# The order of the projection blocks of a differential attention, and a query norm in two halves

## The chip, the cores and the metric

One core of a Trainium2 chip runs the whole program: TensorE (PE) for matmuls and transposes, with its weight loads (PEld), VectorE (DVE), ScalarE (ACT), GpSimd (POOL), and SyncE (SP), which issues nearly all DMAs. The metric is the device time of one execution in microseconds. Before the change it is 2127.65 us, the median of 3 runs (2126.36 to 2130.23).

## The reference

Two models run one after the other on 256 tokens of width 1024, in float32. The first has two layers, each with an FFN, a mixer (a short convolution in layer 0, a sparse attention in layer 1) and a second FFN. The second takes the first one's tokens (the latents, x) and 256 context tokens (ctx, here xc), and has two layers as well. Only its mixers matter here.

```python
# layer 0: differential attention, for latents and context with the same weights
q, k, v = jnp.split(t @ w_in, 3, axis=-1)            # 3 x 1024 columns
q = rmsnorm(q.reshape(Bt, Lt, 16, 64), q_norm)       # per head of 64
k = rmsnorm(k.reshape(Bt, Lt, 16, 64), k_norm)
q = apply_axial_rope(q, cos, sin)                    # latents alone
k = apply_axial_rope(k, cos, sin)
p = jax.nn.softmax(s, axis=-1)                       # two maps for each of 8 heads
a = p[:, :, 0] - lam * p[:, :, 1]
# layer 1: grouped attention, 8 query heads of 128 on 2 key and value heads
q = rmsnorm(q.reshape(Bt, Lt, 8, 128), q_norm)
s = jnp.einsum('bkgtd,bksd->bkgts', qg, keys) * 128 ** -0.5
```

In both the latents attend to context and latents together; the context of layer 0 attends to itself.

## The kernel before, in words

**Tiling.** 256 tokens are two tiles of 128 (`TT = 2`). Every weight is read in float32 (512 KB for half a slab, `raw_half`, line 237), copied to a rounded high part on ACT (line 246) and a remainder on DVE (line 247); a product is three matmuls (high x high, high x remainder, remainder x high). `a_block` multiplies all tokens with 512 columns: two slabs, eight steps over the inner dimension, two accumulators of 128x512 in PSUM, 48 matmuls. PSUM gives six buffers to tag `ps` and two to `fps`.

**The differential projections** (`second`, phase diff0; the loop at line 1344) are six such blocks. Block b has `part, c = divmod(b, 2)`: b = 0, 1 are queries of heads 0 to 7 and 8 to 15, b = 2, 3 keys, b = 4, 5 values. The order is 0, 4, 2, 1, 5, 3. After block b's matmuls the loop calls `flush()` of the block before, which transposes its normed tiles on PE into `qT` or `kT` (`tr_to`, line 981, and a copy on ACT, line 982), and then `diff_block` for b. A value block is two copies on ACT (line 994). For queries and keys `head_norm` (line 946 on) runs for each token tile: a square on ACT (951), a reduction on DVE (952), the factor (382 on DVE, a power on POOL, 386), for keys the multiplication by it (956, DVE), the two rope products (964, and four pieces at 972, DVE) and their sum (974, DVE); without tables one product with the gain (961). A query's factor is applied later, within the softmax. Behind the loop a stretch of filler runs (`self.fd(self.cfg["diff_mid"])`), then the last `flush`, then `diff_attend`, whose first step multiplies queries and keys (line 1038) and reduces the maximum on DVE (1044).

**The context stream** (`ctx_stream`, line 1179 on) is a generator that does the same for xc without tables, in pieces that the main program takes as filler (`fd`, `fa`): by an estimated time at token boundaries (`boundary`), one piece at a time in the FFNs of layer 1. It has the same order of blocks (line 1198). Its tmp and out buffers hold two tiles each. When its attention is done in program order, keys and values are stored to DRAM (lines 1212, 1213) and read back for the latents (1351, 1352). All of them and the weights go out on SP. The conditioning vectors are filler as well: a 512 KB load, then one or two DVE passes over 1024 columns (line 176).

**The grouped attention** (`second`, phase gqa). Queries are two blocks of four heads. The first is normed (`gqa_q(0, acc)`) beside the second one's matmuls, which are a generator `qgen`, run in part ahead of `gqa_attend` and in part at its step n = 1. `gqa_attend` walks 16 pairs of head and token tile: at step n `stage_a` (scores, line 1125; maximum, 1128, exponential on ACT, 1131; scaling, 1133), then, back in the loop of `second`, whatever stands at n, then `stage_b` of n - 2 (transposes, 1143) and for every second n `stage_c` (line 1151). At n = 1 the rest of `qgen` and the norm of both token tiles are queued, at n = 5 the transposes of both into `qT`. Heads 4 to 7 are used from step 8 on.

**What sets the order.** The engines work in order, each through its own queue. The order of a queue is made when the program is built: a scheduler takes the instructions in program order of priority, but lets a later one go ahead where an earlier one is not ready in its own model of time. Weight splits get a bonus of 36 places (`early`). The kernel's text therefore sets the order around the change only nearly.

Of the kernel before, what the change touches and what calls it, by code (L numbers as in the profile page):

```python
# [25 lines left out]
TT = T // P  # L26
# [44 lines left out]
class Slots:  # L71
# [8 lines left out]
    def next(self):  # L80
        self.i += 1
        return self.parts[(self.i - 1) % len(self.parts)]


class Kern:
# [1093 lines left out]
    def ctx_stream(self):  # L1179
        nc, I = self.nc, self.I  # L1180
        tag = "fps"
        yield "d", 2.0
        self.late_setup()
        diags = [self.norm_r(self.xc, t) for t in range(TT)]
        ab = self.ab(("c", 0, 0), ("c", 0, 1), self.n1(0))
        for _ in self.norm_T(self.xc, diags, ab, tag):
            yield "d", 0.5
        h = self.hT
        qT = self.chunk().rearrange("p (h t) -> p h t", h=8)
        kT = self.chunk().rearrange("p (h t) -> p h t", h=8)  # L1190
        vals = self.chunk().rearrange("p (t d) -> p t d", t=TT)
        rq = self.cp.tile([P, TT, 16], F32, name="rqc")
        tmp, outs = Slots(self.chunk(), 512, 4), None
        outs = Slots(tmp.parts[2:4])
        tmp = Slots(tmp.parts[0:2])
        hk = self.tiles_of(h)
        flush = lambda: None
        for b in (0, 4, 2, 1, 5, 3):
            yield from self.a_block(hk, I["diff_w_in"][2 * b:2 * b + 2], tag, ("p", 2.6))
            flush()  # L1200
            flush = self.diff_block(tmp, outs, self.acc2, b, qT, kT, vals, rq, None, "ps")
        for _ in range(3):
            yield "p", 1.3
        flush()
        hid = self.hid8()
        c = self.chunk()
        es = Slots(c[:, 0:1024], T)
        ats = Slots(c[:, 1024:1536], T)
        ons = Slots(c[:, 1536:2048], P)
        yield from self.diff_attend(es, ats, ons, qT, rq, [(kT, vals)], tag, hid)  # L1210
        self.kvd = self.dram.tile([2, P, 2048], F32, name="kvd")
        nc.sync.dma_start(self.kvd[0], kT.rearrange("p h t -> p (h t)"))
        nc.sync.dma_start(self.kvd[1], vals.rearrange("p t d -> p (t d)"))
        yield "d", 1.7
        G = self.grow(("b", 0, 2), i=1)
        for c in range(2):
            yield from self.a_block(hid, I["diff_w_out"][2 * c:2 * c + 2], tag, ("d", 2.6))
            for t in range(TT):
                self.post2(self.xc, [self.acc2[t]], G, t, [c])
        diags = [self.norm_r(self.xc, t) for t in range(TT)]  # L1220
        ab = self.ab(("b", 0, 3), ("b", 0, 4), self.n2(0), i=1)
        yield "d", 1.7
        G = self.grow(("b", 0, 5), i=1)
        for _ in self.norm_T(self.xc, diags, ab, tag):
            yield "d", 1.5
        h = self.hT
        hid = self.hid4()
        win, wout = I["ffn_w_in"][4 * NF:5 * NF], I["ffn_w_out"][44:55]
        for j in range(0, NF, 4):
            n = min(4, NF - j)  # L1230
            for k in range(n):
                yield from self.ffn_in(h, win[j + k], hid[k], tag, ("d", 2.6))
            for c in range(2):
                yield "d", 1.3
                if n == 4:
                    w = self.slab(tuple(wout[j // 2 + s].rearrange("p (k n) -> p k n", k=2)[:, :, c * 512:(c + 1) * 512]
                                        for s in range(2)))
                elif c == 0:
                    w = self.slab(wout[j // 2])
                acc = [self.ps(tag=tag) for _ in range(TT)]  # L1240
                for k in range(n):
                    if k:
                        yield "d", 1.3
                    if n == 4:
                        ww = tuple(z[:, (k % 2) * 512:(k % 2 + 1) * 512] for z in w[k // 2])
                    else:
                        ww = tuple(z[:, c * 512:(c + 1) * 512] for z in w[k])
                    for t in range(TT):
                        self.a_step([acc[t]], hid[k], ww, k == 0, k == n - 1, t)
                for t in range(TT):  # L1250
                    self.post2(self.xc, [acc[t]], G, t, [c])
        g = self.chunk()
        self.gkT = g[:, 0:1024].rearrange("p (h t) -> p h t", h=2)
        self.gv = g[:, 1024:2048].rearrange("p (k d) -> p k d", k=4)
        diags = [self.norm_r(self.xc, t) for t in range(TT)]
        ab = self.ab(("b", 1, 0), ("b", 1, 1), self.n1(1), i=1)
        for _ in self.norm_T(self.xc, diags, ab, tag):
            yield "d", 0.5
        h = self.hT
        yield from self.a_block(self.tiles_of(h), I["gqa_kv"], tag, ("k", 2.6))  # L1260
        c = self.chunk()
        flush = self.gqa_kv(Slots(c[:, 0:1024], 512), Slots(c[:, 1024:2048], 512), self.acc2, self.gkT, self.gv, 0, None, tag)
        yield "d", 0.5
        flush()
# [67 lines left out]
    def second(self, h):  # L1332
# [8 lines left out]
        tmp, outs = Slots(c0, 512), Slots(c1, 512)  # L1341
        hk = self.tiles_of(h)
        flush = lambda: None
        for b in (0, 4, 2, 1, 5, 3):
            acc = self.block(hk, I["diff_w_in"][2 * b:2 * b + 2])
            flush()
            flush = self.diff_block(tmp, outs, acc, b, qT, kT, vals, rq, tabs, "ps")
# [52 lines left out]
        hk = self.tiles_of(h)  # L1400
        flush = self.gqa_kv(tmp, outs, self.block(hk, I["gqa_kv"]), self.gkT, self.gv, T, tabs, "ps")

        def gqa_q(c, acc):
            pend = []
            for t in range(TT):
                rr = rq[:, t, 4 * c:4 * c + 4]
                o = self.head_norm(tmp, outs, acc[t], 4, 128, self.row("gq"), tabs[0], t, rr, False)
                nc.vector.tensor_scalar(rr, rr, 128.0 ** -0.5, None, op0=ALU.mult)
                pend.append((qT[:, 4 * c:4 * c + 4, t * P:(t + 1) * P], o))

            def flush():
                for dst, o in pend:
                    self.tr_to(dst, o, 4)

            return flush

        acc = self.block(hk, I["gqa_q"][0:2])
        flush()
        flush = gqa_q(0, acc)
        qgen = self.a_block(hk, I["gqa_q"][2:4], "ps", ("q", 0.0))  # L1420
        for n, _ in enumerate(qgen):
# [6 lines left out]
        for n, _ in enumerate(self.gqa_attend(es, ats, qT, rq, self.gkT, self.gv, hid)):  # L1428
            if n == 1:
                for _ in qgen:  # L1430
                    pass
                flush = gqa_q(1, self.acc2)
            if n == 5:
                flush()
            if n in (16, 17):
                next(pg)
        got["acc"] = self.proj(pg)
# [122 lines left out]
```

## Time and profile before

| | before |
|---|---|
| median of 3 runs | 2127.65 us |
| the profiled execution | 2128.49 us |
| its span, first to last instruction | 2126.4 us |
| PE, PEld, DVE, ACT, POOL busy | 94%, 84%, 77%, 51%, 7% |
| bytes moved by DMA | 486.45 MB, 229 GB/s in the mean |
| mean granted clock of TensorE | 0.98 |

Busy shares are those of one profiled execution. A matmul's end is modelled, so a busy PE is not PE at its peak. In a timeline a row has start and duration in us, engine, line, operation, the tile written and the tiles read, and in brackets the idle time of the engine ahead of it with what ended it. The number behind a tile's name tells instances apart. Times count from the span's start.

### The profile page before, as it was taken

The numbers are of one execution on the slowest core, as the hardware profiler recorded it, in microseconds if no ns is written. First come the engines' busy times: TensorE is split into PE (matmuls) and PEld (weight loads), VectorE is DVE, ScalarE is ACT, GpSimd is POOL, SyncE is SP. The second block draws the span as 40 slices with busy tenths as digits, with TensorE's granted clock in tenths as the row PEclk, the third lists the DMA queues.
The fourth block names the chain that finished last, engine by engine and source line by source line (L and its number), as shares of the span: only waits on it lengthen the run. The fifth ranks groups of instructions, "written<-read, shape, count | busy, mean of one in ns | idle before, by whom it ended". The sixth has DMA issues, their size and how long they took to land.

```text
span 2126.4 us, 34675 instructions
## 1 busy us (share of the span) xinstructions
PE 2004.0 (94%) x13158; PEld 1791.2 (84%) x13158; DVE 1628.7 (77%) x2753; ACT 1092.4 (51%) x1773; POOL 142.2 (7%) x188
## 2 busy tenths in 40 slices
PE   6999999999899989999999999989999999999998
PEld 5998897998789878887878999868878899768998
DVE  7878899877886778789978667789879755866454
ACT  4444545443454456657755444548754444555443
POOL 0000201000200000110001000210111000100000
PEclk9999999999999999999999999999999999999999
DMA  8989798988677765563677866564458855414553
GB/s 334 329 310 349 244 324 289 330 296 295 221 278 267 270 203 190 187 232 111 225 240 246 261 234 231 171 208 145 144 173 301 277 185 193 163 50 156 188 184 117
DMA packets 136326, 486.45 MB, mean 229 GB/s; under 512 B 14976, under 2 KB 16480, under 8 KB 135392
## 3 DMA queue, kind: packets, MB, share of 16 engines
q1 hardware_dynamic: 134240, 477.90, 65.7%
q0 software_dynamic: 1728, 6.29, 0.9%
q8 instruction: 103, 1.69, 0.3%
q14 instruction: 63, 0.52, 0.1%
q10 hardware_dynamic: 192, 0.05, 0.0%
HBM read 480.47 MB, written 3.19 MB: 227 GB/s over the span
## 4 chain that ended last, share of the span: by engine, by line
PE 57%; DVE 17%; DMA 11%; issue 6%; ACT 5%; POOL 3%; SPq 0%; DVEq 0%; POOLq 0%; ACTq 0%
DMA raw.ctx.1333_7232<-in_diff_w_in 1%; DMA x<-in_x 0%; DVE x L640 0%; DVE xc L648 0%; DMA raw.a02.1070_5840<-in_ada_w 0%; DMA raw.bffn0.3272_17501<-in_ffn_w_in 0%; ACT chunk.diff0.2769_14964 L1048 0%; DMA raw.a01.584_3153<-in_a_w_in 0%; PE ps.a10.1301_7026 L743 0%; DMA raw.ctx.690_3700<-in_diff_w_in 0%; DMA raw.a01.616_3371<-in_a_w_in 0%; DMA raw.ctx.3148_16958<-in_ffn_w_out 0%; DVE chunk.a11.1878_10047 L886 0%; DVE chunk.a11.1878_10047 L864 0%; DMA raw.a02.924_4991<-in_ada_w 0%
## 5 line engine op out<-in xcount | busy, mean ns | idle before, releaser
L1048 ACT ACT_TABLE_LOAD x15 | 19.2, 1283 | 4.1 <-DVE dst.diff0.2773_14978 L1046 2.2
L340 ACT ACT_TABLE_LOAD x16 | 20.5, 1283 | 0.3
L273 PE MATMUL ps.a00.6_101<-ident,x 128*128 128x128 f32 x4 | 1.1, 427 | 13.6 <-DMA x<-in_x 13.6
L375 POOL DMA_DIRECT2D G.a02.1032_5643<-row.a02.1031_5641 x1 | 0.6, 595 | 180.2 <-DMA row.a02.1031_5641<-diag.a02.1030_5639 180.2
L375 POOL DMA_DIRECT2D G.a12.2539_13777<-row.a12.2538_13775 x1 | 0.6, 595 | 178.5 <-DMA row.a12.2538_13775<-diag.a12.2537_13773 178.5
L273 PEld LDWEIGHTS ps.a00.6_101<-ident,x 128*128 128x128 f32 x4 | 0.7, 216 | 13.6 <-issue 13.6
L375 POOL DMA_DIRECT2D G.bffn2.3890_21467<-row.bffn2.3889_21465 x1 | 0.6, 595 | 171.6 <-DMA row.bffn2.3889_21465<-diag.bffn2.3888_21463 171.6
L401 POOL TENSOR_TENSOR rv.ctx.354_2048<-ss.ctx.352_2044,epsd 128x1 f32<-128x1 f32 x1 | 0.2, 189 | 169.4 <-ACT junk.ctx.351_2043 L394 169.4
L375 POOL DMA_DIRECT2D G.bffn0.3422_18599<-row.bffn0.3421_18597 x1 | 0.6, 595 | 150.9 <-DVE wlo.bffn0.3441_18733 L247 150.9
L733 ACT ACTIVATE chunk.a10.1248_6646<-chunk.kv.1128_6071,cols 128x60 f32<-128x60 f32 x32 | 10.1, 390 | 1.0 <-PE ps.a10.1253_6696 L743 1.0
L333 ACT ACT_TABLE_LOAD x8 | 10.3, 1283 | 0.1
L868 ACT ACT_TABLE_LOAD x7 | 9.0, 1283 | 0.1
L386 POOL TENSOR_TENSOR rr.ctx.1408_7659<-rv.ctx.1407_7657,nhalf 128x8 f32<-128x8 f32 x1 | 2.5, 2477 | 93.1 <-DVE rv.ctx.1407_7657 L382 93.1
L375 POOL DMA_DIRECT2D G.a11.2178_11660<-row.a11.2177_11658 x1 | 0.5, 527 | 121.9 <-DMA row.a11.2177_11658<-diag.a11.2176_11656 121.9
L981 PE MATMUL ps.diff0.2763_14946<-ident,chunk.diff0.2627_14248 128*128 128x128 f32 x4 | 1.1, 435 | 7.1 <-DVE chunk.diff0.2627_14248 L974 7.1
L287 PE MATMUL ps.a00.38_198<-chunk.a00.20_148,chunk.a00.34_188 128*128 128x256 f32 x8 | 3.3, 408 | 4.5 <-ACT chunk.a00.34_188 L299 2.9
L484 ACT CAST chunk.a01.490_2583<-chunk.a01.492_2585 128x256 fp32r<-128x256 f32 x8 | 3.3, 407 | 7.8 <-DVE chunk.a01.492_2585 L676 7.7
L981 PEld LDWEIGHTS ps.diff0.2763_14946<-ident,chunk.diff0.2627_14248 128*128 128x128 f32 x4 | 0.7, 218 | 7.5 <-DVE chunk.diff0.2627_14248 L974 7.5
L287 PEld LDWEIGHTS ps.a00.38_198<-chunk.a00.20_148,chunk.a00.34_188 128*128 128x128 f32 x8 | 2.0, 254 | 5.3 <-ACT chunk.a00.34_188 L299 3.1
L1143 PE MATMUL ps.gqa.3570_19374<-ident,chunk.gqa.3552_19276 128*128 128x128 f32 x4 | 1.1, 435 | 5.1 <-DVE chunk.gqa.3552_19276 L1133 5.1
L386 POOL TENSOR_TENSOR rqc<-rv.ctx.1316_7169,nhalf 128x8 f32<-128x8 f32 x1 | 1.6, 1636 | 61.2 <-DVE rv.ctx.1318_7177 L382 61.2
L1143 PEld LDWEIGHTS ps.gqa.3570_19374<-ident,chunk.gqa.3552_19276 128*128 128x128 f32 x4 | 0.7, 217 | 5.9 <-DVE chunk.gqa.3552_19276 L1133 5.9
(11975 smaller groups left out, 9437.3 us busy)
## 6 DMA issues: line engine op xcount, KB each, us to landing
srow<-in_crow SPq DMA_DIRECT2D x3, 512.0 KB, 4.2
x<-in_x SPq DMA_DIRECT2D x1, 1024.0 KB
xc<-in_ctx SPq DMA_DIRECT2D x1, 1024.0 KB
kvd<-chunk.ctx.452_2429 SPq DMA_DIRECT2D x1, 1024.0 KB, 8.2
kvd<-chunk.ctx.451_2428 SPq DMA_DIRECT2D x1, 1024.0 KB
chunk.diff0.2765_14958<-kvd SPq DMA_DIRECT2D x1, 1024.0 KB
chunk.diff0.2766_14959<-kvd SPq DMA_DIRECT2D x1, 1024.0 KB
out<-x SPq DMA_DIRECT2D x2, 512.0 KB, 2.6
```

The lines of the kernel that those rows point to most:

```text
L273: nc.tensor.transpose(ps[:, k, t * P:(t + 1) * P], self.x[:, t, kt * P:(kt + 1) * P], self.ident)
L287: mm(out, whi[:, ks], hi[:, k], start=(k == 0), stop=False)
L333: nc.scalar.activation(sg, gate, AF.Silu)
L340: nc.scalar.activation(sg, gate, AF.Silu)
L375: nc.gpsimd.dma_start(G, src.to_broadcast([P, D]))
L386: nc.gpsimd.tensor_tensor(r, v, self.nhalf[:, 0:n], op=ALU.pow)
L484: nc.scalar.copy(hi, src)
L733: nc.scalar.activation(bt[:, j], self.kv2[i][:, :, 2 * j:2 * j + 16 * (NCMP - 1) + 1:16], AF.Identity, bias=self.col("pos", 16 * i + j, 1))
L868: nc.scalar.activation(p[:, br], p[:, br], AF.Exp, bias=mx[:, par, br:br + 1], accum_out=sm[:, br, par:par + 1])
L981: nc.tensor.transpose(ps[:, j, :], src[:, j * P:(j + 1) * P], self.ident)
L1048: nc.scalar.activation(e[:, :nk], ps[:, :nk], AF.Exp, bias=st[:, m:m + 1], scale=r, accum_out=st[:, 2 + m:3 + m])
L1143: nc.tensor.transpose(pt[:, kb, :], e[:, kb * P:(kb + 1) * P], self.ident)
```

## The change

Both loops over the differential projections take the blocks in the order 0, 2, 4, 1, 3, 5: queries, keys, values, and again. The norm of the second query block of the grouped attention is no longer queued for both token tiles at step 1: tile 0 is normed at step 2 and tile 1 at step 4, and their transposes are queued at steps 5 and 7.

```diff
-        for b in (0, 4, 2, 1, 5, 3):
+        for b in (0, 2, 4, 1, 3, 5):
             yield from self.a_block(hk, I["diff_w_in"][2 * b:2 * b + 2], tag, ("p", 2.6))
             flush()
             flush = self.diff_block(tmp, outs, self.acc2, b, qT, kT, vals, rq, None, "ps")
...
-        for b in (0, 4, 2, 1, 5, 3):
+        for b in (0, 2, 4, 1, 3, 5):
             acc = self.block(hk, I["diff_w_in"][2 * b:2 * b + 2])
...
-        def gqa_q(c, acc):
+        def gqa_q(c, acc, ts=range(TT)):
             pend = []
-            for t in range(TT):
+            for t in ts:
...
             if n == 1:
                 for _ in qgen:
                     pass
-                flush = gqa_q(1, self.acc2)
-            if n == 5:
-                flush()
+            if n == 2:
+                flushes = [gqa_q(1, self.acc2, [0])]
+            if n == 4:
+                flushes.append(gqa_q(1, self.acc2, [1]))
+            if n in (5, 7):
+                flushes.pop(0)()
```

## Rows read from the trace of the kernel before

**Rows 1.** The page: busy us, share of the span and instructions of each engine.
```profile
PE 2004.0 (94%) x13158; PEld 1791.2 (84%) x13158; DVE 1628.7 (77%) x2753; ACT 1092.4 (51%) x1773; POOL 142.2 (7%) x188
```
**Rows 2.** Windows in diff0: length, busy us per engine, clock, DMA share, GB/s.
```profile
1390.00:1402.00 12.00, 11.70 (x55) 9.32 (x54) 11.04 (x24) 5.87 (x8) 3.27 (x2) 1.00 0.75 263
1402.00:1414.00 12.00, 12.00 (x58) 10.00 (x57) 7.44 (x9) 6.46 (x9) 0.00 (x0) 1.00 0.73 224
1414.00:1432.00 18.00, 10.30 (x45) 8.02 (x43) 13.57 (x28) 5.11 (x9) 4.11 (x2) 0.81 0.53 186
1424.70:1430.20 5.50, 4.83 (x14) 3.68 (x15) 4.95 (x11) 1.68 (x3) 0.00 (x0) 0.54 0.14 34
1432.00:1460.00 28.00, 26.33 (x184) 22.21 (x183) 27.54 (x62) 19.46 (x37) 0.85 (x2) 1.00 0.49 162
```
**Rows 3.** Timeline of PE at the end of the projections.
```profile
1424.74 0.48 PE L981 MATMUL ps.diff0.2763_14946<-ident,chunk.diff0.2627_14248 128*128 128x128 f32 x1 [7.08 <-DVE chunk.diff0.2627_14248 L974]
1432.08 0.48 PE L1038 MATMUL ps.diff0.2771_14972<-chunk.diff0.2765_14958,chunk.diff0.2623_14243 64*128 64x256 f32 x1
```
**Rows 4.** Windows in gqa, and PE's wait.
```profile
1864.00:1869.00 5.00, 0.00 (x0) 0.00 (x0) 5.00 (x18) 1.38 (x4) 1.01 (x1) 0.77 0.00 0
1869.00:1873.60 4.60, 4.56 (x13) 3.84 (x14) 3.27 (x6) 1.77 (x5) 0.00 (x0) 0.51 0.49 148
1873.60:1880.40 6.80, 6.56 (x34) 4.53 (x34) 3.97 (x11) 4.42 (x10) 0.00 (x0) 1.00 0.13 54
1869.04 1.12 PE L1143 MATMUL ps.gqa.3570_19374<-ident,chunk.gqa.3552_19276 128*128 128x128 f32 x4 [5.07 <-DVE chunk.gqa.3552_19276 L1133]
```
**Rows 5.** Timeline of DVE in the first key block's norm.
```profile
1383.17 0.68 DVE L964 TENSOR_TENSOR chunk.diff0.2627_14248<-chunk.diff0.2626_14247,chunk.diff0.2622_14229 128x512 f32<-128x512 f32 x1
1383.77 0.89 DVE L972 TENSOR_TENSOR chunk.diff0.2626_14247<-chunk.diff0.2626_14247,chunk.diff0.2622_14229 128x128 f32<-128x128 f32 x4
1384.58 0.68 DVE L956 TENSOR_TENSOR chunk.diff0.2626_14247<-ps.diff0.2668_14446,rr.diff0.2686_14538 128x512 f32<-128x512 f32 x1
1385.18 0.68 DVE L974 TENSOR_TENSOR chunk.diff0.2627_14248<-chunk.diff0.2627_14248,chunk.diff0.2626_14247 128x512 f32<-128x512 f32 x1
```
**Rows 6.** Timeline of DVE and of POOL in the last key block's norm.
```profile
1416.85 1.22 DVE L176 SCALAR_TENSOR_TENSOR vjunk.ctx.2807_15158<-raw.ctx.2784_15035,srow 128x1024 bf16<-128x1024 f32 x1 [2.01 <-DMA raw.ctx.2784_15035<-in_ada_w]
...
1420.89 2.48 POOL L386 TENSOR_TENSOR rr.diff0.2742_14840<-rv.diff0.2741_14838,nhalf 128x8 f32<-128x8 f32 x1 [0.95 <-DVE rv.diff0.2741_14838 L382]
```
**Rows 7.** Timeline of PE: first and last wait for a split in diff0.
```profile
1360.95 0.50 PE L511 MATMUL ps.diff0.2651_14357<-wlo.diff0.2661_14398,chunk.a12.2603_14153 128*128 128x512 f32 x1 [0.45 <-DVE wlo.diff0.2661_14398 L247]
...
1396.85 0.50 PE L511 MATMUL ps.diff0.2707_14659<-wlo.diff0.2717_14700,chunk.a12.2603_14153 128*128 128x512 f32 x1 [0.30 <-DVE wlo.diff0.2717_14700 L247]
```
**Rows 8.** Windows where the context stream's blocks end.
```profile
358.00:366.00 8.00, 5.81 (x39) 4.81 (x39) 7.44 (x16) 3.81 (x9) 0.00 (x0) 1.00 0.53 181
570.00:584.00 14.00, 12.18 (x87) 10.71 (x85) 12.20 (x29) 7.35 (x16) 3.29 (x2) 1.00 0.34 121
...
708.00:720.00 12.00, 12.00 (x80) 10.65 (x78) 7.36 (x11) 5.99 (x8) 0.00 (x0) 1.00 0.89 327
...
762.60:770.00 7.40, 7.35 (x25) 5.64 (x26) 5.42 (x14) 2.02 (x6) 0.00 (x0) 0.50 0.67 214
```
**Rows 9.** Timeline behind the context projections; the page's DMA line of the stores.
```profile
746.66 0.52 PE L981 MATMUL ps.ctx.1431_7783<-ident,chunk.ctx.453_2431 128*128 128x128 f32 x3 [1.31 <-DVE chunk.ctx.453_2431 L961]
762.65 0.66 PE L1062 MATMUL fps.ctx.1451_7888<-ident,chunk.ctx.1434_7791 128*128 128x128 f32 x2 [4.65 <-DVE dst.ctx.1450_7878 L1056]
756.99 1.23 DVE L176 SCALAR_TENSOR_TENSOR vjunk.a10.1509_8162<-raw.a10.1492_8097,srow 128x1024 bf16<-128x1024 f32 x1 [3.26 <-DMA raw.a10.1492_8097<-in_ada_w]
708.44 0.41 SPq L1213 DMA_DIRECT2D kvd<-chunk.ctx.452_2429  x1
751.48 0.42 SPq L1212 DMA_DIRECT2D kvd<-chunk.ctx.451_2428  x1
kvd<-chunk.ctx.452_2429 SPq DMA_DIRECT2D x1, 1024.0 KB, 8.2
```

## Prediction

> **What bounds the kernel now.** I read the page first: TensorE (PE) is busy 94% of the span, VectorE (DVE) 77%, ScalarE (ACT) 51% [rows 1]. So an edit pays only where PE stands still, or where it runs at its lower clock. Next I cut the span into stretches around the three places that the change touches, to see which engine is full in each; then I read PE's idle times in the timeline and followed their releasers.
>
> *Projections of the latents* (phase diff0, 1342 to 1432 us). PE is busy 11.70 of 12 us while blocks with a norm pass by, DVE 11.04 of 12 [rows 2]. In 1402 to 1414, behind the value block b = 5, which has no norm, DVE has only 7.44 us to do and PE is full. Then comes the last block's tail, 1414 to 1432: 18 us with 10.30 of PE work [rows 2]. PE waits 7.08 us there for the last DVE addition of the k norm, and the first score matmul of the attention starts at 1432.08 [rows 3]. Right behind the wait PE runs at a granted clock of 0.54, that is mostly at 1.2 GHz, for 5.5 us [rows 2].
>
> *The grouped attention* (phase gqa). PE waits 5.07 us at 1869.04 for a DVE scaling (line 1133) [rows 4]. DVE is busy 5.00 of 5.00 us in that stretch, with the norm of the second four heads, and afterwards PE runs 4.6 us at clock 0.51. From 1873.6 on DVE has room again (3.97 of 6.8) [rows 4].
>
> *The context stream* runs as filler inside other phases, so its blocks end in odd places: the second at a token boundary (about 356), the third at the next one (about 571), the fifth and sixth inside the FFN of layer 1 (about 708 and 733).
>
> **The change part by part.**
>
> *Norm cost.* One k tile on DVE: the table products start 0.60 apart (1383.17 to 1383.77), the four rotated pieces take 0.81 (to 1384.58), the multiplication by the row factor 0.60 (to 1385.18), the closing addition 0.68 [rows 5]; with a reduction, taken as 0.60 like the other passes over 512 columns, 3.3 us, so 6.6 for a k block. A q block lacks the row factor: 5.4. Without rotation tables, as in the context stream, a k tile is reduction, row factor and gain, 1.8 us: 3.7 for the block. A value block costs DVE nothing; it is two copies on ACT.
>
> *Edit 1, latents.* The norms by position are q, none, k, q, none, k; they become q, k, none, q, k, none. No instruction is added. The last k norm moves from behind the last matmuls to beside them (1402 to 1414), and only copies are left at the end. Ceiling by PE: of its 10.30 us in the tail, 4.83 ran at 0.54; at 1.00 they are 2.6, so the tail holds 8.1 us of work, and 18.0 - 8.1 = 9.9 can go. Ceiling by DVE: from 1402 to 1460 DVE has 7.44 + 13.57 + 27.54 = 48.55 us of work in 58 [rows 2], all of which stays; if it were packed as densely as in 1390 to 1402 (92%) the stretch would take 52.8 (gain 5.2), as densely as in 1432 to 1460 (98%) 49.4 (gain 8.6). What is late next: the k norm's own chain. Within it DVE stood 2.01 us for the load of a conditioning row, and the power on GpSimd (POOL) took 2.48 us at the second tile [rows 6]. Beside block 5's matmuls these waits cost PE nothing until its next weights are split. The new neighbours q/k (twice, where there was one k/q pair) each bring waits like the 0.45 and 0.30 us that PE has now when a split stands behind a norm, three in all [rows 7]: +0.4 each at most. I take -7, bounds -9.9 and -2.
>
> *Edit 1, context stream, boundaries.* The k norm goes from the boundary at 571 to the one at 356; copies and 8 transposes go the other way or along. At 358 to 366 DVE is busy 7.44 of 8 and PE 5.81 [rows 8]: 3.7 more DVE work finds 0.6 us of room, so +3.2, and up to +5 if a POOL wait comes with it, at best 0 if the norm is queued behind the boundary's own operations. At 570 to 584 PE loses 1.82 of 14 us, with DVE at 12.20: at most -1.8 back within it. I take both at these values, +1.4, rounded to +1.5; bounds -1.8 and +5.
>
> *Edit 1, context stream, end.* The k norm moves from 734 to 708, where DVE is busy 7.36 of 12 us and PE 12.00 [rows 8], so it is hidden there; without that room it would cost its 3.7. What goes: PE's wait of 1.31 us for the k norm at 746.66 [rows 9]. What may go: the 4.65 us at 762.65. There PE waits for the first weighting of the stream's attention (DVE), and DVE had stood 3.26 us for a conditioning row whose load went out just ahead of a 1 MB store of the context's keys at 751.48 [rows 9]; PE then ran 7.4 us at 0.50 [rows 8], which costs another 3.7. With the norm gone DVE is some 4 us earlier, and that store goes out some 15 us earlier, away from this load. Upper end 1.31 + 4.65 + 3.7 = 9.7; lower end 0, if another load stops DVE there. A coincidence seldom survives a new order whole: I take half, -5.
>
> *Edit 2.* The second query norm was queued whole, 2 x 2.7 us, between score steps 1 and 2; now half stands behind step 2 and half behind step 4, and the transposes follow at 5 and 7, before the heads 4 to 7 are first used at step 8. Ceiling by PE: 5.07 + 4.56 x (1 - 0.51) = 7.3. Ceiling by DVE, whose work stays: of 16.4 us from 1864 to 1880.4 it is busy 5.00 + 3.27 + 3.97 = 12.24 [rows 4], so at most 4.2. Queued behind each half-norm are the score maxima of the next step, and PE's transposes of the probabilities wait for those. Worst end: each half makes its own wait of 2.7 us with the same clock loss, 5.4 + 2.2 against 7.3, so +0.3; one accumulator also stays two steps longer. I take -3, nearest to DVE's ceiling, with a wait of about 1 us left.
>
> *Sum.* -7 + 1.5 - 5 - 3 = -13.5. The profiled execution took 2128.49 us (span 2126.4 and 2.1 around it), 0.84 over the median of the runs and inside their spread: 2115.0.
>
> **Rivals.**
>
> *The attention gives it back* (DVE is the bound after the projections): 27.54 of 28 us busy [rows 2] speaks for it, DVE's 4.4 idle us of 18 in the tail against. The latents then gain 2 instead of 7: -8.5, 2120.
>
> *Waits only change places.* Edit 2 gains nothing (+0.3), the stop at 762 stays (0), the boundary costs 1.5 and the latents give 5: -3.2, 2125.3. For: DVE works in order and is 77% busy [rows 1], and each engine's order is dealt anew when the program changes, so fresh collisions appear. Against: the three stalls named are the largest of their phases.
>
> *Everything goes:* -9 - 4.2 - 9.7 + 0 = -23, 2105.5. For it: PE's ceilings. Against: DVE's.
>
> *Slower: both context stores at once.* Now the store of the values goes out at 708.44 and that of the keys at 751.48 [rows 9]; in the new order keys and values are both finished after the sixth block, and 2 MB go out at about 735. One store takes 8.2 us to land [rows 9]. If weight loads issued behind the pair land 16.4 us late, PE stands that long and pays the 3.7 of the lower clock; the -5 is lost: -13.5 + 5 + 16.4 + 3.7 = +11.6, 2140. It decides from the point at which the loads come later than their lead. Against it: the stretch behind the store at 708 has PE busy 12.00 of 12 us [rows 8]. The Trainium skill, "DMA: Bandwidth & Descriptors", section "Two DMAs through the same engine are not ordered", says that within one queue of an engine descriptors start in order but overlap; by its first half the loads would queue behind both stores, which is this rival, by its second they hardly notice, which is the row at 708. No run here yet shows two stores together.
>
> *Slower: DVE falls behind in the q/k pairs* so far that PE's clock falls: a block is 48 matmuls, of which 58 fill 12 us in 1402 to 1414 [rows 2], so some 10 us; at 1.2 GHz it costs 10 more, two blocks 20, in all +6.5, 2134.5. It decides where waits grow from 0.45 to about the 4.65 us behind which rows 8 show 0.50; rows 2 show 1.00 in the pair that exists (1390 to 1402).
>
> **How the numbers follow.** Forecast 0.48 (its own range 2109 to 2120), everything goes 0.13, the attention gives it back 0.14: faster 0.75. Waits change places 0.14: the same, that is within 0.2% (4.3 us), about what these runs can tell. Stores 0.06 and pairs 0.05: slower 0.11. The range 2105 to 2130 leaves out the slower cases, a little of the third and a little of the fourth.
>
> **What would show it.** Right: the wait of 7.08 gone, the first score matmul of diff0 about 7 us nearer to the start of the first block, clock 1.00 before it; in gqa one or two waits of about 1 us in place of 5.07, clock 1.00; no wait for a k norm near 747 and at most 2 us at the first weighting; one or two more us of PE idle near 360 and less near 580. Wrong: a wait of over 3 us for the third or sixth k tile's addition at the transposes, PE idle in 1432 to 1460 (shifted) grown by several us, or PE waiting for weights behind the two stores.

## The result, and the profile after

The changed kernel takes 2098.33 us, the median of 4 runs (2097.37 to 2100.32), beside 2127.98 for the kernel before: ratio 0.9856, 95% interval 0.9842 to 0.9869, so 29.7 us less where 13.5 were forecast, and outside the range. Run again on another chip the ratio was 0.9882 (0.9858 to 0.9906).

The page's first line answers to [rows 1]: PE has lost 6.4 us of busy time and 23 us of idle time.

```profile
PE 1997.6 (95%) x13158; PEld 1787.6 (85%) x13158; DVE 1628.4 (78%) x2753; ACT 1095.2 (52%) x1775; POOL 142.4 (7%) x188
```

To find the place I cut both spans at the first PE row of each stage. The lengths, in us, of one execution each:

| stage | before | after | difference | forecast |
|---|---|---|---|---|
| a00, a01 (to 357) | 356.8 | 358.0 | +1.2 | 0 |
| a02 (FFN; starts and ends at a token boundary) | 215.1 | 205.7 | -9.4 | +3.2 |
| kv | 54.7 | 48.0 | -6.7 | -1.8 |
| a10 (FFN; end of the context stream and its attention) | 294.7 | 291.7 | -3.0 | -5 |
| a11, a12 | 420.8 | 419.6 | -1.2 | 0 |
| diff0 (projections, attention) | 249.8 | 248.0 | -1.8 | -7 |
| bffn0 | 231.0 | 227.7 | -3.3 | 0 |
| gqa | 108.7 | 102.2 | -6.5 | -3 |
| bffn2 | 188.7 | 189.8 | +1.1 | 0 |

How far two executions differ is seen where kernels have the same order of instructions in a stage: a02 took 214.7 to 219.2 us in six kernels that leave that stage as it was before, a10 287.5 to 292.3 in six that have the changed order of the context stream. So a difference of a few us in one row is not told from that spread.

More than half of the gain, 16 us, lies in a02 and kv, to which the forecast gave +1.4 in sum. Windows over these two stages, before (length, busy us of PE, PEld, DVE, ACT, POOL, clock, DMA share, GB/s):

```profile
356.80:571.85 215.05, 206.41 (x1392) 189.87 (x1391) 164.86 (x222) 96.08 (x123) 8.74 (x13) 0.98 0.84 291
571.85:626.54 54.69, 49.78 (x308) 43.71 (x308) 45.41 (x75) 24.05 (x37) 3.29 (x2) 1.00 0.74 269
```

and after:

```profile
358.03:563.70 205.67, 202.74 (x1401) 188.59 (x1399) 170.88 (x231) 95.86 (x120) 13.01 (x15) 1.00 0.86 303
563.70:611.69 47.99, 47.57 (x307) 42.38 (x305) 41.37 (x67) 24.18 (x39) 0.00 (x0) 1.00 0.86 307
```

In a02 VectorE (DVE) does 6 us *more* after the change, PE's idle time falls from 8.6 to 2.9 us, the clock from 0.98 rises to 1.00, and the same weights come at 303 GB/s instead of 291. What changed is how long DVE waits for conditioning loads at the head of its queue: the bracketed times of the passes (line 176) in a02 add up to 44.9 us (29 waits) before and 12.4 (13 waits) after. The worst one before, in the timelines of DVE, SP and PE and a window:

```profile
536.53 1.22 DVE L247 TENSOR_TENSOR wlo.a02.1058_5791<-raw.a02.1056_5788,whi.a02.1057_5790 128x1024 fp32r<-128x1024 f32 x1
543.40 1.23 DVE L176 SCALAR_TENSOR_TENSOR vjunk.a02.1073_5846<-raw.a02.1070_5840,srow 128x1024 bf16<-128x1024 f32 x1 [5.65 <-DMA raw.a02.1070_5840<-in_ada_w]
...
544.55 1.22 DVE L247 TENSOR_TENSOR wlo.a02.1061_5797<-raw.a02.1059_5794,whi.a02.1060_5796 128x1024 fp32r<-128x1024 f32 x1
```
```profile
526.84 0.33 SPq L237 DMA_DIRECT2D raw.a02.1059_5794<-in_ffn_w_out  x1
...
535.50 0.33 SPq L237 DMA_DIRECT2D raw.a02.1070_5840<-in_ada_w  x1
```
```profile
545.83 0.80 PE L511 MATMUL ps.a02.722_3847<-wlo.a02.1061_5797,chunk.a02.967_5273 128*128 128x512 f32 x1 [2.90 <-DVE wlo.a02.1061_5797 L247]
```
```profile
545.80:549.40 3.60, 3.57 (x9) 2.85 (x10) 3.56 (x6) 0.49 (x1) 0.00 (x0) 0.54 0.86 261
```

The weights `raw.a02.1059` went out at 526.84; their split is due. But the pass for `raw.a02.1070`, whose load went out 8.7 us later, stands ahead of it on DVE. DVE waits 5.65 us, PE 2.90 for the split, and then runs 3.6 us at a clock of 0.54, mostly at 1.2 GHz. I counted this in the order of the two queues: how many weight splits whose loads were issued earlier stand behind each conditioning pass. In a02 it is 2.2 a pass before and 1.1 after, and after the change 0 for the first 14 of 50 passes.

In kv SP itself stands still. A copy of the first kv product (line 710) has to wait for that product, and before the change it heads SP's queue, ahead of loads. SP's waits and timeline, and PE, before:

```profile
SPq L710 <- ACT chunk.kv.1127_6068 L707: 13.5, 1, 13.5
```
```profile
570.20 0.33 SPq L237 DMA_DIRECT2D raw.kv.1162_6250<-in_ada_w  x1
583.54 0.56 SPq L710 DMA_DIRECT2D chunk.kv.1128_6071<-chunk.kv.1127_6068  x1
...
588.20 0.54 SPq L237 DMA_DIRECT2D raw.kv.1166_6306<-in_kv_b  x1
```
```profile
593.77 0.39 PE L492 MATMUL ps.kv.1176_6326<-chunk.a02.1106_5996,whi.kv.1167_6308 128*128 128x256 f32 x1 [1.52 <-ACT whi.kv.1167_6308 L246]
```

SP's timeline after:

```profile
563.71 0.33 SPq L237 DMA_DIRECT2D raw.kv.1168_6318<-in_kv_b  x1
567.09 0.33 SPq L237 DMA_DIRECT2D raw.kv.1171_6324<-in_kv_b  x1
...
575.92 0.64 SPq L710 DMA_DIRECT2D chunk.kv.1130_6083<-chunk.kv.1129_6080  x1
```

Before, no load of weights goes out between 570.2 and 588.2; that is the DMA share of 0.34 at 570 to 584 in [rows 8]. The product itself is not later than after the change: its copy goes out 11.7 us behind the stage's start before (571.85) and 12.2 after (563.70). What differs is SP's order: after the change five loads, two of them the next weights (kv_b), stand ahead of the copy. PE's idle time in the stage falls from 4.9 to 0.4 us; 3.0 of the 4.9 are three stops (1.52, 0.76, 0.76) for the weights that were loaded behind the copy. In the nine kernels with a norm at 571 the copy stands ahead of these weights and kv takes 53.2 to 55.0 us; in the eight without it they go out first, and kv takes 47.5 to 48.6. No run moved the copy by itself. The prediction took from [rows 8] only PE's 1.82 us within the window, and not the loads that were missing 10 us later.

The three places that the prediction named, after the change: PE and DVE in the timeline (answering to [rows 3], [rows 4], [rows 6] and [rows 9]), and windows:

```profile
748.49 0.44 PE L1062 MATMUL fps.ctx.1451_7888<-ident,chunk.ctx.1434_7791 128*128 128x128 f32 x2 [1.06 <-ACT chunk.ctx.1434_7791 L1048]
...
1355.54 0.50 PE L511 MATMUL ps.diff0.2673_14471<-wlo.diff0.2683_14512,chunk.a12.2603_14153 128*128 128x512 f32 x1 [1.52 <-DVE wlo.diff0.2683_14512 L247]
...
1408.48 0.64 PE L510 MATMUL fps.ctx.2763_14950<-whi.ctx.2758_14940,chunk.ctx.1968_10458 128*128 128x512 f32 x1 [2.89 <-DVE xc L648]
...
1840.18 0.66 PE L1143 MATMUL ps.gqa.3570_19374<-ident,chunk.gqa.3552_19276 128*128 128x128 f32 x4 [1.62 <-DVE chunk.gqa.3552_19276 L1133]
```
```profile
1404.26 1.23 DVE L176 SCALAR_TENSOR_TENSOR vjunk.ctx.2807_15158<-raw.ctx.2784_15035,srow 128x1024 bf16<-128x1024 f32 x1 [2.47 <-DMA raw.ctx.2784_15035<-in_ada_w]
```
```profile
748.40:756.00 7.60, 7.51 (x61) 7.04 (x61) 7.60 (x23) 5.02 (x14) 0.00 (x0) 1.00 0.77 223
...
1400.00:1425.00 25.00, 20.30 (x99) 15.84 (x98) 20.35 (x38) 10.46 (x16) 0.00 (x0) 0.86 0.53 191
...
1840.00:1844.60 4.60, 4.42 (x24) 3.45 (x25) 4.60 (x18) 3.27 (x8) 1.17 (x1) 1.00 0.00 0
```

The stop of 4.65 us at the first weighting is 1.06 now, that of 5.07 in gqa 1.62, both with the clock at 1.00. In diff0 the 7.08 us are gone, but the same conditioning load that cost DVE 2.01 us in [rows 6] costs it 2.47 here, holds the context's addition (line 648) behind it, and PE stops 2.89 us at 1408 and falls to a low clock again (0.86 over 25 us). Parted at the first score matmul (1432.08 before, 1404.02 after), diff0 shows where its gain went. Windows before, then after:

```profile
1342.02:1432.08 90.06, 81.17 (x371) 65.81 (x369) 67.69 (x133) 41.60 (x55) 13.91 (x8) 0.96 0.57 190
1432.08:1591.84 159.76, 149.90 (x995) 127.95 (x995) 133.47 (x290) 112.37 (x219) 16.00 (x23) 1.00 0.47 155
```
```profile
1322.98:1404.02 81.04, 79.01 (x370) 64.27 (x368) 65.24 (x129) 41.79 (x55) 13.49 (x8) 1.00 0.58 195
1404.02:1571.02 167.00, 153.19 (x995) 130.19 (x994) 136.98 (x295) 112.47 (x218) 16.92 (x23) 0.98 0.47 157
```

The projections are 9.0 us shorter, and the attention behind them is 7.2 longer: PE has 3.3 us more to do in it and 4.0 more of idle time.

### The profile page after: what moved, and what is told of

Same layout as the page of the kernel before. It is cut to its first block, busy times and chain, and to the rows that moved or that the text cites. A ratio compares the mean times of both kernels' runs of the same rounds, so it can differ in the third digit from the quotient of the medians.

```text
span 2097.0 us, 34670 instructions
## 1 busy us (share of the span) xinstructions
PE 1997.6 (95%) x13158; PEld 1787.6 (85%) x13158; DVE 1628.4 (78%) x2753; ACT 1095.2 (52%) x1775; POOL 142.4 (7%) x188
## 4 chain that ended last, share of the span: by engine, by line
PE 71%; DVE 11%; ACT 5%; DMA 5%; issue 4%; POOL 3%; SPq 0%; DVEq 0%; POOLq 0%; ACTq 0%
DMA x<-in_x 0%; DVE x L640 0%; ACT chunk.diff0.2769_14964 L1048 0%; PE ps.a10.1303_7038 L743 0%; DVE xc L648 0%; DMA raw.kv.1194_6453<-in_kv_v 0%; ACT L1048 0%; DMA raw.ctx.2784_15035<-in_ada_w 0%; PE ps.a10.1255_6708 L743 0%; DMA raw.ctx.2154_11553<-in_ada_w 0%; DMA raw.a10.1460_7906<-in_ada_w 0%; DMA raw.a01.506_2613<-in_a_w_in 0%; ACT chunk.ctx.1434_7791 L1048 0%; DMA raw.bffn0.3160_16986<-in_ffn_w_in 0%; DMA raw.bffn0.3272_17501<-in_ffn_w_in 0%
## 5 line engine op out<-in xcount | busy, mean ns | idle before, releaser
L974 DVE TENSOR_TENSOR chunk.diff0.2627_14248<-chunk.diff0.2627_14248,chunk.diff0.2626_14247 128x512 f32<-128x512 f32 x8 | 5.5, 687 | 0.0
```

Of the source, the lines that this page charges most:

```text
L974: nc.vector.tensor_tensor(o, o, o2, op=ALU.add)
```

## The experiments

All ratios are to the kernel before, run beside it on the same chip; in brackets the 95% interval. A difference behind a ratio is the ratio's, in us.

**One edit at a time.** `e1`: the context stream's order alone; `e2`: the latents' alone; `e3`: the split of the query norm alone; `e8`: the changed kernel with the latents' order put back.

```diff
e1 (line 1198), e2 (line 1344):
-        for b in (0, 4, 2, 1, 5, 3):
+        for b in (0, 2, 4, 1, 3, 5):
e8 (line 1344 of the changed kernel):
-        for b in (0, 2, 4, 1, 3, 5):
+        for b in (0, 4, 2, 1, 5, 3):
```

> Kernel before with the context stream's order alone changed to (0, 2, 4, 1, 3, 5). Theory A (read from the two traces): the stages from the end of a01 to the start of a10 hold the surprise. PE's length from 356.8 to 571.8 falls from 215 to about 206, that of kv from 54.7 to about 48, and the stretch in which the stream ends and attends from 171.5 to about 167; in all -17 us, 2111 us. Theory B (the prediction's terms): the norm only changes its place (+1.5) and the end of the stream gains 5, so 2124.5 us. Between them 2118 decides.

> Kernel before with the latents' order alone changed. The prediction's term is -7 us (2121 us). Theory A, from the lengths of the stages in the two traces: diff0 254.5 to 251.2, so -3.3 us (2124.7 us), and where the 7.08 us stop went the attention gives half back; the shortening of bffn0 by 3.3 us comes with this edit only if that stage's 2.82 us stop at 1674.59 goes too, which would make it 2121.4 us.

> Kernel before with the split of the second query norm alone. The prediction's term is -3 us (2125 us). From the stages' lengths (108.8 to 102.2) it would be -6.6 us (2121.4 us). If part of those 6.6 us came from what the other two edits leave in the queues, it is between the two.

> The changed kernel with the latents' order put back to (0, 4, 2, 1, 5, 3). If that edit is worth what it measured alone (-1.7 us with an interval that holds 0), this one stands within 3 us of the changed kernel: 2099 to 2102 us, with the 7 us stop back in diff0 and the waits of 1.5, 2.9, 1.8 and 2.25 us gone. The prediction's term would make it 2105 us.

Measured: `e1` 2103.94, 0.9889 [0.9873, 0.9904], so -23.6; `e2` 2125.75, 0.9992 [0.9983, 1.0002], -1.7; `e3` 2122.73, 0.9988 [0.9975, 1.0000], -2.6; `e8` 2096.93, 0.9856 [0.983, 0.9881], as the changed kernel. So the context stream brings nearly all, and the latents' edit nothing that can be told from zero. Theory A was right on the place and too low on the size (-17). In `e3` the gqa stage fell to 103.8; it is 102.1 to 103.8 in every kernel with the split and 107.2 to 110.5 in all others. In the kernels with the split the stage behind it, bffn2, is 0.6 to 1.2 us longer. The 3.3 us of bffn0 belong to no edit: with the filler in place that stage takes 226.0 to 230.3 in the other kernels, with and without each edit; 231.0 before was its longest.

**The halves of the context stream's order.**

```diff
e6 (line 1198):
-        for b in (0, 4, 2, 1, 5, 3):
+        for b in (0, 2, 4, 1, 5, 3):
e7 (line 1198):
-        for b in (0, 4, 2, 1, 5, 3):
+        for b in (0, 4, 2, 1, 3, 5):
```

> Kernel before with the context stream's order (0, 2, 4, 1, 5, 3): the first three blocks as in the changed kernel, the last two as before, so a norm still ends the stream. Theory A: a02 -9, kv -7, and the end as before with its stops of 1.3 at 747 and 4.65 at 763 (by the old clock): -16 us, 2111 us. If the end's gain hung on the earlier stages and not on what the last block is, those stops are gone here too: 2104 us as with the whole order.

> Kernel before with the context stream's order (0, 4, 2, 1, 3, 5): only the last two blocks are swapped. The prediction's term for the stream's end, alone: -5 us (2122 us), the 4.65 us stop at the first weighting gone or under 2 us, a02 and kv as before (215 and 54.7). If with the late a10 of the old order the stop stays, 2127 us.

Measured: `e6` 2108.33, 0.9903 [0.9882, 0.9924], -20.6; a02 205.9, kv 47.5, and the end's stops are there, 1.97 us and 4.63 us. `e7` 2121.96, 0.9977 [0.9961, 0.9993], -4.9; a02 214.7, kv 54.4, the stop at the first weighting 1.06. The halves add up (-25.5 beside the -23.6 of `e1`): their gains lie in separate stages. The prediction's -5 for the stream's end is right in size.

**Is it the norm, its place or the order it leaves behind?** `e4` puts the values first, so that a norm (of queries) stands at 356 and the key norm stays at 571. `e5` keeps the old order and only adds work.

```diff
e4 (line 1198):
-        for b in (0, 4, 2, 1, 5, 3):
+        for b in (4, 0, 2, 1, 5, 3):
e5 (behind line 1201):
             flush = self.diff_block(tmp, outs, self.acc2, b, qT, kT, vals, rq, None, "ps")
+            if b == 4:
+                for t in range(TT):
+                    self.head_norm(tmp, outs, self.acc2[t], 8, 64, self.row("dk"), None, t, None, True)
```

> Kernel before with the context stream's order (4, 0, 2, 1, 5, 3): the values stand first, the query norm comes at the end of a01 (about 356) and the key norm stays at the end of a02 (about 571). Theory A1 (what a02 gains is the place of the conditioning passes in VectorE's queue, which a norm at 356 changes: fewer of them stand ahead of weight splits whose loads were issued earlier, 1.4 a pass against 2.2 before and 1.1 after): a02 gets shorter by 6 to 9 us (about 207 in place of 215, and VectorE waits some 15 to 20 us for conditioning loads there in place of 44.9), kv stays at 54 to 55 with its norm, total -7, 2121 us. Theory A2 (both gains come from the norm no longer standing at 571): a02 and kv as before, total within 2 us of 2128. Theory B (a norm costs where it stands): a02 +1 from the norm at its start, 2129 us.

> Kernel before in its old order; behind the values' block (about 356) the key norm's arithmetic runs once more, on the values' sums and into scratch tiles that nothing reads: work is only added, for VectorE some 10 us. Theory A1 (a burst on VectorE at the start of a02 re-deals its queue, and the conditioning passes then stand behind the weight splits of earlier loads: 1.0 such splits a pass behind it against 2.2 before): a02 gets 8 us shorter in spite of the added work, VectorE's waits for conditioning loads there fall from 44.9 to 12 to 16 us, kv stays at 54 to 55; total -6 to -8 us, 2120 us. Theory B (a norm costs where it stands): +1 to +5 us, 2130 us. Theory A2 (only the norm's absence at 571 helps): +1, as B.

Measured: `e4` 2116.27, 0.9957 [0.9944, 0.997]; a02 206.6, DVE's waits there 16.1 us, kv 54.3. `e5` 2115.64, 0.9948 [0.993, 0.9967]; a02 204.9, waits 9.9 us, kv 54.8. The added norm is less than the expectation said, 4.4 us of DVE (two tiles of 0.67, 0.16, 0.69 and 0.69), spread over 362 to 372, with two squares on ACT and two powers on POOL. Still: a kernel with a whole key norm *more* is 11 us faster. So a02 gains from a norm at its start, whichever it is and even a useless one, and kv from the absence of one at 571; theories A2 and B fall.

**The order alone.** Both might still be the burst itself: while DVE is busy, loads run ahead. `e9` adds no work and changes no loop. It only ties each conditioning pass in a02 behind the last weight split whose load was issued before the pass's own. `e10` does this in the changed kernel in all stages.

```diff
         ins = self.nc.vector.tensor_tensor(lo[:, :width], src, ...)      # split, line 247
+        self.last_lo = (self.ph, ins.ins)
...
-        return self.raw_half(src[j]), j, key, conds, vs                  # fetch
+        return self.raw_half(src[j]), j, key, conds, vs, self.last_lo
...
+            with self.tc.issue_after(lo[1]) if lo and self.ph in FORCE else nullcontext():
                 nc.vector.scalar_tensor_tensor(junk, raw, 1.0, ...)      # the pass, line 176
```

> Kernel before, with no work added, moved or taken away: in stage a02 alone each conditioning pass is queued on VectorE behind the last weight split whose load was issued before its own (an order-only edge), so no pass stands ahead of an older split (0 instead of 2.2). Theory A1 (VectorE's order is what a02 gains by): a02 8 to 10 us shorter (205 to 207), VectorE's waits for conditioning loads there from 44.9 to 15 us or less, kv unchanged; total -8 to -11 us, 2116 us. Theory A3 (the burst itself matters: while VectorE is busy with a norm the loads run ahead, whatever the order): a02 stays within 2 us of 215, total 2126. A third way: passes held back keep their load buffers longer, the weight loads come later and a02 gets slower.

> The changed kernel with the same order edge in all stages from a02 to diff0, the context stream's steps among them. If passes that wait at the head of VectorE's queue are also what gave the latents' gain back (the 2.47 us wait for raw.ctx.2784 at 1401.8, and behind it the 2.89 us stop of PE at 1408 with the halved clock), those go: diff0 -4 to -5, a02 -1 to -2, the rest as it is: 2092 us. If passes held back only keep load buffers longer, 2098 to 2103 us.

Measured: `e9` 2113.2, 0.9955 [0.9937, 0.9973], -9.6; a02 206.2, kv 55.0. The stage's window, and the pass that had waited 5.65 us (its load now goes out at 527.21, not 535.50; line numbers are 5 or 6 higher):

```profile
354.86:561.08 206.22, 202.51 (x1392) 187.77 (x1390) 169.37 (x224) 96.07 (x124) 8.76 (x13) 1.00 0.85 305
```
```profile
536.26 1.23 DVE L252 TENSOR_TENSOR wlo.a02.1069_5837<-raw.a02.1067_5834,whi.a02.1068_5836 128x1024 fp32r<-128x1024 f32 x1 [0.20 <-ACT whi.a02.1068_5836 L251]
...
538.01 1.22 DVE L181 SCALAR_TENSOR_TENSOR vjunk.a02.1073_5846<-raw.a02.1070_5840,srow 128x1024 bf16<-128x1024 f32 x1
```

No pass in a02 waits for its load any more, and PE's stops of 2.21 and 2.90 us there are gone. SP issues the same loads in the same order as in the kernel before, and on DVE the passes and splits have changed places. Theory A1 is shown: a02's gain is the order of DVE's queue. A3 falls.

`e10` measured 2100.59, 0.9892 [0.987, 0.9915], no better than the changed kernel. In a12 the forced order took away all of DVE's waits for conditioning loads (28.7 us in the kernel before, 22.4 and 30.6 in two executions of the changed one), and the stage stayed at 206.8 (207.4, 206.0 and 206.2). Diff0 stood at 244.8, against 248.0 and 245.3 in the changed kernel: the stop at 1408 shrank to 0.70 us, but one of 3.54 for another of the context's additions came at 1474. In a10 the stage took 281.7 us, against 287.5 to 292.3 in the six kernels named above. In a11 the edge cost 10 to 15 us (228.3, against 213.6 and 217.9): DVE works without a gap from 1061 to 1072, and passes that were held back come in a row there, three from 1067.1 to 1070.9, ahead of the context's feed-forward. The two stages together take 510.0 us, and 505.3 and 510.1 in the changed kernel. PE in a11:

```profile
1013.48 0.79 PE L516 MATMUL fps.ctx.2053_10940<-whi.ctx.2045_10924,chunk.ctx.1968_10458 128*128 128x512 f32 x1 [3.23 <-DVE sg.ctx.2041_10905 L347]
...
1071.33 0.80 PE L516 MATMUL fps.ctx.2157_11559<-whi.ctx.2149_11543,chunk.ctx.1968_10458 128*128 128x512 f32 x1 [4.11 <-DVE sg.ctx.2145_11524 L347]
```

Why do 45 us of waits cost 9 in a02, and some 30 nothing in a12? By the count above the order is no better in a12: 2.7 earlier splits a pass. The window of a12 before:

```profile
1134.65:1342.02 207.37, 202.99 (x1435) 191.28 (x1434) 152.73 (x198) 95.06 (x123) 7.87 (x13) 0.99 0.73 249
```

Busy and waiting together fill DVE to 152.7 + 28.7 = 181 of 207 us in a12, and to 164.9 + 44.9 = 210 of 215 in a02. Only there was no room left. That this sum decides is argued from two stages and not shown, and a10 does not fit it: DVE is busy or waiting 230 + 14 = 244 of 291.7 us there in the changed kernel, and yet the edge made that stage 6 to 11 us shorter.

**Where the latents' gain went.** With the values last nothing waits at the end of the projections, but 8 us of context work (`diff_mid`) are still called up there, and it was in this work that PE stopped at 1408. `e11` is the changed kernel without it, `e14` the latents' order alone without it, `e15` the old order without it, `e13` the changed kernel without it and with the order edge of `e9` in a02; `e12` is the changed kernel again, on the chip of `e13` to `e15`.

```diff
- 'diff_mid': 8.0,
+ 'diff_mid': 0.0,
```

> The changed kernel without the 8 us of context work that is called up between the latents' last block and their attention (it was there to cover the norm that ended that stretch). Theory C (with the values last the filler covers nothing, and its feed-forward waits on VectorE behind a conditioning load, 2.89 us at 1408): that stop goes, diff0 -3, 2095 us. Theory D (the attention's start has the same wait for VectorE and lacks that filler later): 0 to +3 us, 2098 to 2101.

> The changed kernel as it is, to stand beside the next three on one chip: ratio 0.985 to 0.987 by all that was measured of it; the sum of its parts measured alone (0.9889, 0.9992 and 0.9988 multiplied) is 0.987.

> The changed kernel without the 8 us of context work ahead of the latents' attention, and with the order edge of the conditioning passes in stage a02 alone. From the parts: the missing filler was worth some 7 us against the changed kernel in the stages' lengths, the order edge takes VectorE's remaining 12 us of waits in a02, of which PE shows at most 2.9 us idle: ratio 0.982, 5 to 9 us under the changed kernel, 2089 us. If the norm at 356 had already brought all that the order can give, it is the filler alone: 0.983.

> Kernel before with the latents' new order and without the filler. Theory C (the edit gave back its gain because the filler, called up where nothing waits any more, puts context work and its VectorE waits ahead of the attention): about 10 us better than the latents' order with the filler, ratio 0.994 to 0.995. Theory E (the filler is bad in either order and the latents' order brings nothing): the same as the next kernel, the old order without the filler.

> Kernel before, without the filler, in its old order. Theory C: PE waits for the last key norm with nothing between, the 7.08 us stop becomes about 12 to 14 us (the norm's length from its block's last matmul), diff0 loses 2 to 6 us against what the later stages win: ratio 0.998 to 1.003, clearly above the kernel with the new order and no filler. Theory E: as that one, 0.994 to 0.996.

| kernel | median us | ratio |
|---|---|---|
| `e11` changed, no filler | 2090.20 | 0.9844 [0.9821, 0.9867] |
| `e12` changed | 2100.79 | 0.9882 [0.9858, 0.9906] |
| `e13` changed, no filler, order edge | 2085.50 | 0.9812 [0.9788, 0.9836] |
| `e14` latents' order, no filler | 2114.04 | 0.9947 [0.9932, 0.9962] |
| `e15` old order, no filler | 2124.28 | 0.9990 [0.9974, 1.0006] |

Neither the latents' order (0.9992) nor the missing filler (0.9990) is worth anything alone that can be told from zero; together they are 0.9947, -11.3 us. In the times theory C holds and E falls. For the changed kernel itself the missing filler alone is not clear of the noise (0.9844 beside 0.9856 and 0.9882). Windows over the whole of diff0, `e14`:

```profile
1343.65:1572.94 229.29, 218.95 (x1303) 183.90 (x1301) 193.12 (x411) 147.74 (x267) 28.05 (x31) 0.99 0.51 176
```

and `e15`:

```profile
1348.66:1583.46 234.80, 219.71 (x1303) 184.58 (x1302) 191.51 (x409) 145.63 (x265) 30.64 (x31) 0.99 0.50 170
```

PE is idle 10.3 us in the one and 15.1 in the other (18.8 in the kernel before). Some of the stage's 20 us moves on: bffn0 takes 234.1 to 234.8 us without the filler, with the context work that it takes over, and 226.0 to 231.0 with it.

The traces bear theory C out only in part. Of the 11.6 us between the two executions, 5.5 lie in diff0 and 5.0 ahead of it, where the queues of both kernels hold the same instructions in the same order. And in `e15` the stop of 7.08 us did not grow to 12 to 14, as expected: it is gone. Context work stands ahead of the last transposes there all the same, and the longest stop in diff0 is this:

```profile
1438.36 0.50 PE L510 MATMUL fps.ctx.2784_15029<-whi.ctx.2779_15019,chunk.ctx.1968_10458 128*128 128x512 f32 x1 [3.19 <-DVE xc L648]
```

Diff0 and bffn0 together are 11.9 us shorter in `e15` than in the kernel before, though its time is the same; a02 took 219.0 us in that execution, with the order of the kernel before. What takes the 11.9 us back is open.

`e13` is the fastest kernel of the study: 15.3 us under the changed kernel on the same chip and 40.6 under the kernel before. How much of the 15.3 is the order edge is not known: a02 was 206.7 us with it and 205.8 without.

## Why the prediction was wrong, point by point

**The context stream's boundaries (+1.5): this step failed.** It said that the norm "finds 0.6 us of room" at 358 to 366, "so +3.2", and at 571 "at most -1.8 back within it". It measured -20.6 (`e6`, of which a02 and kv show 16.4 in their lengths). The price of the norm was not what mattered: the rest of a02 and kv, beyond the windows at the two boundaries, was held fixed, and the bounds (-1.8 to +5) were drawn from two windows of 8 and 14 us. Two things were missing. In a02 DVE was 97.5% busy or waiting, and the waits came from the order in which the build deals its queue (shown by `e9`); a norm at the stage's start deals that order anew (`e4`, `e5`). In kv the build put the copy of the first product ahead of the next weight loads on SP wherever a norm stood at 571; that the norm's place decides it is shown by `e1` and `e4` to `e7`, the way through SP's order is read from the traces. That a useless norm at the same place does it too (`e5`) says that a02's part is luck and not a merit of the new order.

**The latents (-7): right at its place, and lost behind it.** The 7.08 us went, as forecast, and the first score matmul starts 81.0 us into the stage in place of 90.1: 9.0 us, near the ceiling of 9.9. But -1.7 [-3.6, +0.4] remained of it. The step that failed is that the attention's length would stay: it grew by 7.2 us. That is the prediction's own rival, "the attention gives it back", which had a chance of 0.14. By "DVE is the bound" it is not explained, with DVE busy 137.0 of the 167.0 us: without the filler the order is worth 2124.3 - 2114.0 = 10 us, 5.5 of them in diff0. So filler that had lost its purpose has a part in it. The conditioning load ahead of the stop at 1408 is not the cause by itself: `e10` took away its wait, and diff0 gained 0.5 to 3.2 us. How the rest comes about is open.

**The stream's end (-5): right.** It measured -4.9 [-8.3, -1.5] in `e7`; the stop of 4.65 us became 1.06, the one of 1.31 is gone, and DVE no longer waits for `raw.a10.1492`. `e6`, where a norm still ends the stream, kept both stops.

**The split (-3): right.** It measured -2.6 [-5.3, 0], with one named wait of 1.62 us in place of 5.07, clock 1.00. The stage's 5 to 6.5 us are nearer to the ceiling by PE (7.3) than to that by DVE (4.2); about 1 us of them is lost again in bffn2.

**The rivals.** "Waits only change places" had the fact that decided, "each engine's order is dealt anew", and took it for a source of losses alone. "Everything goes" was meant as the outer end and was passed, because nothing outside the named stops was in it. The two stores did not meet; SP's timeline and a window after:

```profile
725.66 0.42 SPq L1212 DMA_DIRECT2D kvd<-chunk.ctx.451_2428  x1
733.86 0.78 SPq L1213 DMA_DIRECT2D kvd<-chunk.ctx.452_2429  x1
```
```profile
732.00:748.00 16.00, 14.25 (x82) 11.21 (x80) 12.01 (x23) 10.01 (x14) 0.00 (x0) 1.00 0.92 325
```

They went out 8.2 us apart, and PE lost 1.75 us of 16 behind them at a clock of 1.00. The Trainium skill, "DMA: Bandwidth & Descriptors", section "Two DMAs through the same engine are not ordered", says that descriptors in one queue of a DMA engine start in order but are pipelined. The 1.75 us that PE lost agree with that, but no run here had both stores out at once. DVE did not fall behind in the pairs of queries and keys: one wait of 1.52 us at 1355.54.

**Its sums.** Two are a little off: 3.7 - 0.6 is 3.1 and not 3.2, and the case of the pairs ends at 2135.0 and not 2134.5. Nothing hangs on either.

## What to carry to other kernels

When an operation moves, its price is not all that changes: the queues of the stages behind its old and its new place are dealt anew. Ahead of pricing it, add for each such stage an engine's busy time and its waits; the stage in which they filled the length (a02) answered by more than the operation costs, though one stage here (a10) did not keep to that. Where a queue's order comes from a model, look on every queue, SP's too, for instructions that wait while work that is ready stands behind them, and tie them down in that stage alone: the same edge brought nothing in a12 and starved another stream in a11. When an edit removes a wait, measure it also without the filler that was put there to cover the wait.

## What the runs showed that was not expected

A kernel with a useless norm more (4.4 us on DVE) and nothing else changed was 11 us faster (`e5`, 0.9948). And 22 to 31 us of DVE waits for loads in one stage could go without moving its length by 1 us (`e10`, a12), while 44.9 in a stage of the same kind cost 9 (`e9`, a02).
